# Latent attention scores as three pairs of 64-row products on the two halves of TensorE

## The chip, the cores and the metric

The kernel runs on one core of a Trainium2 chip. The metric is the device time of one execution in microseconds (us), as the median of several. A core has engines that each run their own stream of instructions in order: TensorE (PE in the profile, with its weight loads shown apart as PEld), VectorE (DVE), ScalarE (ACT), GpSimd (POOL) and SyncE (SP), which here issues all DMA transfers. TensorE multiplies a stationary operand, the weights, that is loaded into its array of 128 rows by 128 columns, with a moving operand that is streamed through, and adds up in PSUM. The array's rows are the summed index of a product.

## The reference, cut to what matters

Two layers of a block over 1024 latent and 256 context tokens. In each layer a differential attention runs over 4 heads with 2 maps each (m below), with heads of 64 numbers; its scores, softmaxes and values are what the change touches:

```python
def diff_attention(q, k, v, lam):
    # q (B,Lq,H,2,64), k (B,Lk,H,2,64), v (B,Lk,H,128)
    def one_block(qblk):                      # 128 queries
        s = jnp.einsum('bqhmd,bkhmd->bmhqk', qblk, k).astype(jnp.float32) * scale
        p = jax.nn.softmax(s, axis=-1)
        w = p[:, 0] - lam * p[:, 1]
        return jnp.einsum('bhqk,bkhd->bqhd', w.astype(v.dtype), v)
...
k_all = jnp.concatenate([kc, kx], axis=1)     # 256 context keys, 1024 latent keys
ax = rms_norm(diff_attention(qx, k_all, v_all, lam), p['g_subln']) * (1.0 - lam_init)
...
if ctx_out:                                   # layer 0 only
    ac = rms_norm(diff_attention(qc, kc, vc, lam), p['g_subln']) * (1.0 - lam_init)
```

All inputs are float32. The rest of a layer (one input projection, a state-space scan, a Fourier mixer, an output projection and an MLP) isn't touched.

## The kernel before

The program is one long stretch per stage: input projection, attention, output projection, MLP, twice. Nearly all products of the large stages split each float32 operand into a rounded part (high) and its remainder (low) and multiply these in the one-pass type fp32r, three products for one.

Queries and keys leave the input projection as such pairs. `stack` transposes a block of them, splits it and writes it to DRAM: KD[h, e] holds the keys of head h, part e (0 high, 1 low), with 64 rows of map 0 and 64 rows of map 1, over 1280 columns (1024 latent keys, then 256 context keys); QD[t, e] holds the queries of block t of 128.

The attention reads them back. `load_k(h)` fills two tiles of 128 rows and 1280 columns, ST[h][m] for map m: rows 0 to 63 hold the high part of its keys, rows 64 to 127 the low part. `load_q(t)` fills QS[0] (high) and QS[1] (low), each with the same 64 rows twice, in rows 0 to 63 and 64 to 127. So a product of QS[e] with ST[h][m] over all 128 rows sums the query's part e with both parts of the keys, and two products (e = 0 and 1, `product`, line 654) give all four combinations.

`scores` is called for every block t and head h. It makes the context scores C of both maps (four products of 256 columns), then for each map the latent scores S (line 654 again: two halves of 512 keys, two products each, so four of 512 columns). S is one of two PSUM tiles of two banks, one bank for each half. VectorE takes the maximum over S (line 668), ScalarE the exponential with a running sum (line 670 for S, line 671 for C). `combine` weighs the two maps (line 682, in layer 1 partly on GpSimd, lines 684 and 685). `values` turns the result with ten transposes (line 696), which ScalarE copies out (line 697), and multiplies with V (line 700, float32, so that each of the ten products shows as two in the trace); `finish` (line 714) transposes the outputs. Values lag the scores by three heads. Layer 0 has eight full blocks and two of context queries alone, layer 1 has eight: 2 x 8 x 4 x 2 = 128 maps with latent scores in all.

Beside it run, as fill, the state-space output (`glu`, line 1090, which reads HD back from DRAM, line 1081, after it was written at line 1057) and, in layer 0, part of a modulation product (lines 419 and 427).

Each engine's order is set by a list scheduler, which works over the whole program with costs and dependences; instructions whose costs or number change can come to stand in another order. PE's order is fixed in the program: when its next instruction waits, all behind it wait. SP issues its DMAs in order too.

Elsewhere in the program the state-space setup (lines 917 and 919) already has products of 64 rows, line 917 on rows 0 to 63, line 919 on rows 64 to 127, and line 921 products of 128 rows.

Of the kernel before, what the change touches and what calls it, by code (L numbers as in the profile page):

```python
# [13 lines left out]
F32 = mybir.dt.float32  # L14
# [9 lines left out]
SEQ = 1024  # L24
CTX = 256
TOK = SEQ + CTX
# [41 lines left out]
class Block:  # L68
# [561 lines left out]
    def attention(self, l, V):  # L630
        nc = self.nc
        ST = []

        def load_k(h):
            ST.append([self.s5([128, TOK], F32R) for _ in range(2)])
            for m in range(2):
                for e in range(2):
                    nc.sync.dma_start(ST[h][m][e * 64:e * 64 + 64].bitcast(F32), self.KD[h, e, m * 64:m * 64 + 64])

        def load_q(t, pool='qs'):  # L640
            QS = [self.tl(pool, [128, 2, 4, 128], F32R) for _ in range(2)]
# [7 lines left out]
        def scores(h, t, QS, n):  # L649
            full = t < 8  # L650

            def product(dst, m, a, b):
                for e in range(2):
                    nc.tensor.matmul(dst, QS[e][:, m, h], ST[h][m][:, a:b], start=(e == 0), stop=(e == 1))  # L654

            C = self.pb((128, 2, CTX))
            for m in range(2):
                product(C[:, m], m, SEQ, TOK)
            mx = self.psmall([128, 2, 2], 'mx', 4)
            sm = self.psmall([128, 2, 2], 'es', 5)  # L660
            nc.vector.tensor_reduce(mx[:, :, 0], C, AX.X, ALU.max, negate=True)  # L661
            PR = [E[m][n % 4] for m in range(2)]
            for m in range(2):
                if full:
                    S = self.tl('s', [128, SEQ])
                    for a in (0, 512):
                        product(S[:, a:a + 512], m, a, a + 512)
                    nc.vector.tensor_reduce(mx[:, m, 1:2], S, AX.X, ALU.max, negate=True)  # L668
                    nc.vector.tensor_tensor(mx[:, m, 0:1], mx[:, m, 0:1], mx[:, m, 1:2], ALU.min)  # L669
                    nc.scalar.activation(PR[m][:, 0:SEQ], S, AF.Exp, bias=mx[:, m, 0:1], accum_out=sm[:, m, 1:2])  # L670
                nc.scalar.activation(PR[m][:, SEQ:TOK], C[:, m], AF.Exp, bias=mx[:, m, 0:1], accum_out=sm[:, m, 0:1])
            if full:
                nc.vector.tensor_tensor(sm[:, :, 0], sm[:, :, 0], sm[:, :, 1], ALU.add)  # L673
            return PR, sm
# [43 lines left out]

        pend, done = [], []
        load_k(0)  # L720
        order = range(8) if l == DEPTH - 1 else (0, 1, 2, 8, 3, 4, 9, 5, 6, 7)
        nxt = load_q(0, 'w4')
        for h in range(1, NH):
            load_k(h)
# [3 lines left out]
        for i, t in enumerate(order):  # L728
            QS = nxt
            if i + 1 < len(order):  # L730
                nxt = load_q(order[i + 1])
            AX4 = self.tl('ax' if i + 1 < len(order) else 't2', [128, 4, 128])
            ssq = self.psmall([128, 4], 'ssq', 3)
            for h in range(NH):
                old = pend.pop(0) if len(pend) > 2 else None
                if old is not None:
                    w = combine(*old[:4])
                pend.append((h, t, *scores(h, t, QS, i * NH + h), AX4, ssq, i * NH + h))
                if old is not None:
                    values(*old[:2], *w, *old[4:])  # L740
                if h == 2 and len(done) > 1:
                    finish(*done.pop(0))
                yield
            done.append((t, AX4))
# [698 lines left out]
```

## Time and profile before

| | us |
|---|---|
| median of 3 runs | 3052.49 (3051.86 to 3054.81) |
| the profiled execution, its own time | 3055.69 |
| span of its trace | 3053.9 |
| PE busy | 2907.2 (95%) |
| DVE busy | 1977.9 (65%) |
| ACT busy | 1069.1 (35%) |
| POOL busy | 592.6 (19%) |

The span runs from the first to the last instruction. Busy time is the union of an engine's instructions; matmuls are pipelined, so that one shows some 0.39 us from start to end though the next starts 0.23 us after it. Times between the starts of instructions that follow each other are therefore what counts on PE. The latent scores run from 435 to 684 us (layer 0) and from about 2030 to 2228 us (layer 1).

### The profile page before, as it was taken

The page shows a single profiled execution, that of the slowest core. Times are in us where ns is not written, and L with a number is a line of the kernel's source. Part 1 is how long each engine was busy: PE and PEld are TensorE (multiplying, and loading weights), DVE is VectorE, ACT ScalarE, POOL GpSimd, SP SyncE. Part 2 cuts the span into 40 slices and gives each one's busy share as a digit, 9 for nine tenths or more (in the row PEclk, how much of TensorE's full clock was granted, in tenths as well). Part 3 has the DMA queues.
Part 4 walks back from the last instruction along what each step waited for, and adds up shares of the span by engine and source line. Part 5 has one row for each costly group of instructions (what it writes and reads, how often), then busy time and mean ns, then how long its engine had stood idle before and what let it go on. Part 6 is the DMA issues. An engine that isn't in the chain of part 4 may idle for free. (4 is left out here: it accounts for less than half of the span.)

```text
span 3053.9 us, 40975 instructions
## 1 busy us (share of the span) xinstructions
PE 2907.2 (95%) x15277; PEld 2407.3 (79%) x15277; DVE 1977.9 (65%) x3547; ACT 1069.1 (35%) x2371; POOL 592.6 (19%) x516
## 2 busy tenths in 40 slices
PE   6889989999999999999999999889999999999999
PEld 2557768778888888888888777768889888888887
DVE  7866857785586776775455547858866554455444
ACT  5324437674321211212212433438853222212222
POOL 0643520010100000000465213526621000000000
PEclk9899999999999999999999999999999999999999
DMA  8355483535022322322222235471250111111111
GB/s 291 118 155 158 144 208 121 158 97 162 28 90 78 95 76 83 98 69 61 63 80 70 106 99 153 147 175 49 50 155 29 55 42 56 49 49 42 56 49 66
DMA packets 280851, 299.93 MB, mean 98 GB/s; under 512 B 47158, under 2 KB 191948, under 8 KB 280652
## 3 DMA queue, kind: packets, MB, share of 16 engines
q1 hardware_dynamic: 280652, 297.31, 32.5%
q8 instruction: 120, 1.97, 0.3%
q14 instruction: 79, 0.65, 0.1%
HBM read 229.31 MB, written 67.93 MB: 97 GB/s over the span
## 5 line engine op out<-in xcount | busy, mean ns | idle before, releaser
L1269 PE MATMUL b_t<-hid_t,w_t 128*128 128x512 f32 (+1 forms) x3840 | 809.3, 370 | 0.0
L1246 PE MATMUL b_t<-s_t,w_t 128*128 128x512 f32 (+1 forms) x3840 | 800.4, 369 | 0.0
L1269 PEld LDWEIGHTS b_t<-hid_t,w_t 128*128 128x128 f32 x3840 | 669.6, 189 | 121.8 <-issue 1.9
L1246 PEld LDWEIGHTS b_t<-s_t,w_t 128*128 128x128 f32 x3840 | 669.0, 188 | 121.3 <-issue 1.1
L1271 DVE SCALAR_TENSOR_TENSOR kv_t<-b_t,mod,kv_t 128x512 f32<-128x512 f32 (+1 forms) x640 | 439.4, 694 | 236.6 <-PE b_t L1269 235.6
L159 ACT CAST w_t<-r_t 128x512 fp32r<-128x512 f32 x336 | 195.0, 619 | 807.7 <-PE b_t L1269 526.2
L160 DVE TENSOR_TENSOR w_t<-r_t,w_t 128x512 fp32r<-128x512 f32 x328 | 232.5, 736 | 219.5 <-ACT w_t L159 218.9
L589 PE MATMUL b_t<-w_t,s_t 128*128 128x512 f32 (+1 forms) x1392 | 355.6, 410 | 19.5 <-DVE t_t L478 6.7
L589 PEld LDWEIGHTS b_t<-w_t,s_t 128*128 128x128 f32 x1392 | 264.9, 197 | 83.2 <-issue 9.7
L133 POOL TENSOR_TENSOR sm<-sm,mhalf 128x8 f32<-128x8 f32 (+3 forms) x66 | 103.4, 1567 | 569.6 <-DVE sm L540 191.6
L1250 DVE TENSOR_TENSOR t_t<-b_t,t_t 128x512 f32<-128x512 f32 x160 | 101.2, 633 | 135.6 <-ACT t_t L1249 135.2
L897 POOL TENSOR_TENSOR bg_t<-pt_t,bw_t 128x256 f32<-128x256 f32 x56 | 43.3, 773 | 741.1 <-DMA bw_t<-BD 656.9
L700 PE MATMUL b_t<-kv_t,kv_t 128*128 128x128 f32 x1312 | 178.0, 280 | 3.9 <-ACT kv_t L697 3.4
L700 PEld LDWEIGHTS b_t<-kv_t,kv_t 128*128 128x128 f32 x1312 | 164.2, 193 | 15.0 <-ACT kv_t L697 9.3
L668 DVE TENSOR_REDUCE mx<-s_t 128x1 f32<-128x1024 f32 x128 | 155.2, 1218 | 27.0 <-PE s_t L654 26.5
L159 ACT CAST hid_t<-t_t 128x512 fp32r<-128x512 f32 x160 | 92.4, 578 | 214.0 <-DVE t_t L1250 213.9
L1249 ACT ACTIVATE t_t<-b_t 128x512 f32<-128x512 f32 x160 | 88.3, 552 | 202.3 <-PE b_t L1246 202.3
L670 ACT ACTIVATE s_t<-s_t,mx 128x1024 f32<-128x1024 f32 x128 | 143.6, 1122 | 36.6 <-DVE mx L669 29.0
L160 DVE TENSOR_TENSOR hid_t<-t_t,hid_t 128x512 fp32r<-128x512 f32 x160 | 106.8, 667 | 66.2 <-ACT hid_t L159 66.2
L654 PE MATMUL s_t<-s_t,qs_t 128*128 128x512 f32 x448 | 132.8, 419 | 13.4 <-ACT s_t L670 8.5
L381 DVE SCALAR_TENSOR_TENSOR ac_t<-bg_t,vc,ac_t 128x512 f32<-128x512 f32 x168 | 118.8, 744 | 36.0 <-DMA bg_t<-in_w_mod_dram 35.8
L616 PE MATMUL b_t<-w_t,s_t 128*128 128x512 f32 x480 | 115.6, 395 | 6.7 <-DVE w_t L160 3.5
(335 smaller groups left out, 3506.5 us busy)
## 6 DMA issues: line engine op xcount, KB each, us to landing
r_t<-in_w_ff_dram SPq DMA_DIRECT2D x256, 256.0 KB
bg_t<-in_w_mod_dram SPq DMA_DIRECT2D x96, 256.0 KB
r_t<-in_w_in_dram SPq DMA_DIRECT2D x64, 256.0 KB
qs_t<-QD SPq DMA_DIRECT2D x64, 256.0 KB
XD<-kv_t SPq DMA_DIRECT2D x16, 640.0 KB
KD<-t_t SPq DMA_DIRECT2D x40, 256.0 KB
s_t<-KD SPq DMA_DIRECT2D x32, 320.0 KB
QD<-t_t SPq DMA_DIRECT2D x36, 256.0 KB
```

The source lines that it names most:

```text
L159: self.nc.scalar.copy(h, raw)
L160: (eng or self.nc.vector).tensor_tensor(l, raw, h, ALU.subtract)
L381: nc.vector.scalar_tensor_tensor(acc[v], w, c, acc[v], ALU.mult, ALU.add)
L589: nc.tensor.matmul(p[:, :cols], a[:, ts], W[k][:, b, :cols], start=(n == 0), stop=(n == 23))
L616: nc.tensor.matmul(p, a[:, ts], W[k][:, b], start=(n == 0), stop=(n == 11))
L654: nc.tensor.matmul(dst, QS[e][:, m, h], ST[h][m][:, a:b], start=(e == 0), stop=(e == 1))
L668: nc.vector.tensor_reduce(mx[:, m, 1:2], S, AX.X, ALU.max, negate=True)
L670: nc.scalar.activation(PR[m][:, 0:SEQ], S, AF.Exp, bias=mx[:, m, 0:1], accum_out=sm[:, m, 1:2])
L700: nc.tensor.matmul(o, WT[:, kt * 128:(kt + 1) * 128], V[kt // 5][:, kt % 5, h * 128:(h + 1) * 128], start=(c == 0), stop=(c == len(ks) - 1))
L1246: nc.tensor.matmul(p[:, :w], W[a][:, k], b[k][:, s:s + w], start=(q == 0), stop=(q == 23))
L1269: nc.tensor.matmul(p[:, :w], W[a][:, cs], hid[b][:, s:s + w], start=(q == 0), stop=(q == n - 1))
L1271: nc.vector.scalar_tensor_tensor(xs, p[:, :w], self.mod[l][:, 40 + c, g // 2:g // 2 + 1], xs, ALU.mult, ALU.add)
```

## The change

The latent scores of a map are made of products over 64 rows instead of 128. Per map there are three pairs: query high with key high, query low with key high, query high with key low. The combination of the two low parts, which the kernel before includes, is left out. In each pair the first product uses rows 0 to 63 of the array on keys 0 to 511, the second rows 64 to 127 on keys 512 to 1023; they write the two banks of S. That makes six instructions of 512 columns where there were four, and they are kept in this order.

The keys are laid out for it: of ST[h][e] rows 0 to 63 now hold part e of both maps for latent keys 0 to 511 (map 0, then map 1), rows 64 to 127 the same for keys 512 to 1023. The context columns stay as they were, and so do the context scores. Each of the four loads of a head becomes two: one of 64 rows with two pieces of 512 columns, one of 64 rows with 256 columns.

```diff
         def load_k(h):
             ST.append([self.s5([128, TOK], F32R) for _ in range(2)])
-            for m in range(2):
-                for e in range(2):
-                    nc.sync.dma_start(ST[h][m][e * 64:e * 64 + 64].bitcast(F32), self.KD[h, e, m * 64:m * 64 + 64])
+            for e in range(2):
+                src = self.KD[h, e].rearrange('(m d) c -> d m c', m=2)
+                for r in range(2):
+                    rows = slice(r * 64, r * 64 + 64)
+                    nc.sync.dma_start(ST[h][e][rows, 0:SEQ].rearrange('d (m c) -> d m c', m=2).bitcast(F32),
+                                      src[:, :, r * 512:r * 512 + 512])
+                    nc.sync.dma_start(ST[h][r][e * 64:e * 64 + 64, SEQ:TOK].bitcast(F32), src[:, r, SEQ:TOK])
...
-            def product(dst, m, a, b):
-                for e in range(2):
-                    nc.tensor.matmul(dst, QS[e][:, m, h], ST[h][m][:, a:b], start=(e == 0), stop=(e == 1))
+            def latent(S, m):
+                for q, (e, f) in enumerate(((0, 0), (1, 0), (0, 1))):
+                    for r in range(2):
+                        rows = slice(r * 64, r * 64 + 64)
+                        ins = nc.tensor.matmul(S[:, r * 512:r * 512 + 512], QS[e][rows, m, h],
+                                               ST[h][f][rows, m * 512:m * 512 + 512], start=(q == 0), stop=(q == 2))
+                        if q or r:
+                            self.tc.keep_in_program_order(ins)

             C = self.pb((128, 2, CTX))
             for m in range(2):
-                product(C[:, m], m, SEQ, TOK)
+                for e in range(2):
+                    nc.tensor.matmul(C[:, m], QS[e][:, m, h], ST[h][m][:, SEQ:TOK], start=(e == 0), stop=(e == 1))
...
                     S = self.tl('s', [128, SEQ])
-                    for a in (0, 512):
-                        product(S[:, a:a + 512], m, a, a + 512)
+                    latent(S, m)
```

The scheduler's order moves with it, on PE, DVE and ACT within the two attention stages and on SP at their start. On PE in the middle of layer 1, from the end of one map's latent scores (S, s_t) over ten transposes (line 696, idn) and a head's value products (line 700, kv_t) to the next head's context scores (b_t, 128x256), the rows before are

```order
L654 MATMUL s_t_18933<-s_t_17975,qs_t_18434 128x512
L654 MATMUL s_t_18933<-s_t_17975,qs_t_18435 128x512
L696 MATMUL b_t_18943<-idn_141,s_t_17980 128x128 x2
L696 MATMUL b_t_18947<-idn_141,s_t_17980 128x128 x4
L696 MATMUL b_t_18953<-idn_141,s_t_17980 128x128 x4
L700 MATMUL b_t_18943<-kv_t_17644,kv_t_17988 128x128 x2
L700 MATMUL b_t_18943<-kv_t_17489,kv_t_17988 128x128 x4
L654 MATMUL b_t_18986<-s_t_17950,qs_t_18703 128x256
```

and in the changed program, where all lines from 638 on have moved (654 is 660 for the latent scores and 668 for the context scores, 696 is 705, 700 is 709):

```order
L660 MATMUL s_t_19155<-s_t_18130,qs_t_18626 128x512 x2
L660 MATMUL s_t_19155<-s_t_18130,qs_t_18627 128x512 x2
L660 MATMUL s_t_19155<-s_t_18131,qs_t_18626 128x512 x2
L705 MATMUL b_t_19167<-idn_141,s_t_18140 128x128 x2
L705 MATMUL b_t_19171<-idn_141,s_t_18140 128x128 x4
L705 MATMUL b_t_19177<-idn_141,s_t_18140 128x128 x4
L660 MATMUL s_t_19218<-s_t_18094,qs_t_18911 128x512 x2
L660 MATMUL s_t_19218<-s_t_18094,qs_t_18912 128x512 x2
L660 MATMUL s_t_19218<-s_t_18095,qs_t_18911 128x512 x2
L709 MATMUL b_t_19167<-kv_t_17788,kv_t_18148 128x128 x2
L709 MATMUL b_t_19167<-kv_t_17633,kv_t_18148 128x128 x4
L668 MATMUL b_t_19210<-s_t_18094,qs_t_18911 128x256
```

A map's six products stand together between work of 128 rows, and the next head's first map now comes ahead of the value products and of its own context scores. In the whole program the 768 products of 64 rows stand in 121 such groups, 112 of them with one map, 54 of them followed by a transpose of line 696.

On SP at the start of the attention of layer 0, where the keys of head 0 (s_t) are loaded ahead of the first queries (w_t), before:

```order
L638 DMA s_t_3868<-KD 64x1280 x2
L638 DMA s_t_3869<-KD 64x1280 x2
L646 DMA w_t_3874<-QD 64x2x512 x2
L646 DMA w_t_3875<-QD 64x2x512 x2
L638 DMA s_t_3880<-KD 64x1280 x2
```

and now, the last part of the same stretch:

```order
L642 DMA s_t_3869<-KD 64x256
L640 DMA s_t_3869<-KD 64x2x512
L642 DMA s_t_3868<-KD 64x256
L640 DMA s_t_3869<-KD 64x2x512
L642 DMA s_t_3869<-KD 64x256
L650 DMA w_t_3878<-QD 64x2x512 x2
L650 DMA w_t_3879<-QD 64x2x512 x2
L640 DMA s_t_3884<-KD 64x2x512
```

Eight loads stand where four did, for each of four heads in each layer, with the same bytes; the rest of SP's order there is the same.

## Rows read from the trace of the kernel before

**Rows 1.** The page's part 1: busy us, share of the span, instructions.

```profile
PE 2907.2 (95%) x15277; PEld 2407.3 (79%) x15277; DVE 1977.9 (65%) x3547; ACT 1069.1 (35%) x2371; POOL 592.6 (19%) x516
```

**Rows 2.** Windows, both attention stages: length, busy per engine, granted clock, DMA share, GB/s.

```profile
core 0: us, PE busy (x) PEld busy (x) DVE busy (x) ACT busy (x) POOL busy (x), PEclk, DMA share, GB/s
450.00:700.00 250.00, 231.50 (x1618) 192.17 (x1617) 197.74 (x399) 183.91 (x496) 20.49 (x18) 0.99 0.41 123
2060.00:2230.00 170.00, 164.36 (x1188) 149.84 (x1187) 148.99 (x293) 141.72 (x375) 111.72 (x69) 0.99 0.20 51
```

**Rows 3.** The chain that ended last, layer 1's attention (2060 to 2230 us), by line.

```profile
by line: PE b_t L700 27.8%; PE s_t L654 23.0%; PE b_t L696 11.3%; DVE mx L668 7.8%; PE b_t L654 6.1%; issue 4.6%; DVE s_t L682 4.1%; ACT s_t L670 3.6%; DVE es L673 3.2%; DVE mx L661 2.5%; DVE mx L669 1.6%; PE b_t L714 1.5%; DVE s_t L160 1.0
```

**Rows 4.** Waits of PEld, 430 to 720 us: total us, times, longest.

```profile
PEld s_t L654 <- ACT s_t L670: 11.5, 20, 1.1
```

**Rows 5.** Waits of PEld, 2040 to 2250 us.

```profile
PEld s_t L654 <- ACT s_t L670: 7.9, 10, 1.6
```

**Rows 6.** Timeline of PE, layer 1: start us, us, line, operation, tiles, shape, count.

```profile
2125.62 1.04 PE L696 MATMUL b_t<-idn,s_t 128*128 128x128 f32 x8
2126.41 1.17 PE L654 MATMUL s_t<-s_t,qs_t 128*128 128x512 f32 x4
2127.42 1.50 PE L700 MATMUL b_t<-kv_t,kv_t 128*128 128x128 f32 x12
2128.75 0.60 PE L714 MATMUL b_t<-idn,ax_t 128*128 128x128 f32 x4
```

**Rows 7.** Groups by form, whole span: count, busy us, mean ns, idle before.

```profile
L1269 PE MATMUL b_t<-hid_t,w_t 128*128 128x512 f32 x3072 | 715.2, 392 | 0.0
```

**Rows 8.** Timeline of PE, state-space setup beside the input projection, layer 0.

```profile
120.17 0.62 PE L589 MATMUL b_t<-w_t,s_t 128*128 128x512 f32 x2
120.73 0.36 PE L917 MATMUL f_t<-bg_t,bw_t 64*16 64x112 f32 x2
...
121.84 0.94 PE L919 MATMUL f_t<-bg_t,bw_t 64*16 64x112 f32 x8
122.71 0.21 PE L921 MATMUL f_t<-bw_t 128*16 128x16 f32 x2
```

**Rows 9.** The same, a little earlier, where lines 917 and 919 alternate.

```profile
117.74 0.27 PE L917 MATMUL f_t<-bg_t,bw_t 64*16 64x112 f32 x1
117.75 0.27 PE L919 MATMUL f_t<-bg_t,bw_t 64*16 64x112 f32 x1
117.85 0.26 PE L917 MATMUL f_t<-bg_t,bw_t 64*16 64x112 f32 x1
117.86 0.26 PE L919 MATMUL f_t<-bg_t,bw_t 64*16 64x112 f32 x1
...
118.43 0.50 PE L589 MATMUL b_t<-w_t,s_t 128*128 128x512 f32 x1
```

**Rows 10.** Line 654's own view, latent scores: ns shortest/median/longest.

```profile
L654 PE MATMUL s_t<-s_t,qs_t x448: 387/397/774, 467.2 to 2227.3; 128*128 128x512 f32 x150
```

**Rows 11.** Timeline of PE: transposes right after a product of 64 rows.

```profile
104.71 0.26 PE L919 MATMUL f_t<-bg_t,bw_t 64*16 64x112 f32 x1
104.89 0.66 PE L910 MATMUL f_t<-idn,bg_t 128*128 128x128 f32 x4
```

**Rows 12.** Timeline of SP, start of layer 0's attention: start us, us, DMA issues.

```profile
403.23 15.39 SPq L638 DMA_DIRECT2D s_t<-KD  x12
...
422.85 5.99 SPq L646 DMA_DIRECT2D qs_t<-QD  x5
429.71 8.70 SPq L1057 DMA_DIRECT2D HD<-kv_t  x8
```

**Rows 13.** Timeline of PE there; in brackets idle us before, and its releaser.

```profile
444.71 2.08 PE L1090 MATMUL b_t<-kv_t,w_t 128*128 128x512 f32 x2 [7.29 <-DMA kv_t<-HD]
```

**Rows 14.** Windows, layer 1: a stretch and the one after it (columns as in rows 2).

```profile
2068.10:2071.50 3.40, 1.37 (x7) 1.05 (x8) 2.86 (x7) 2.38 (x7) 1.29 (x2) 1.00 0.01 2
2071.50:2074.90 3.40, 3.40 (x17) 3.12 (x16) 3.00 (x5) 2.21 (x6) 2.73 (x2) 0.51 0.00 0
```

## The prediction

> **What bounds the kernel now.** The page's shares come first: PE is busy 95% of the span and no other engine over 65% [rows 1], so work taken from PE counts unless the stage has another limit. The change lies in two stages, and the windows over them say which: in layer 1 PE is busy 164.4 of 170 us, DVE 149.0, ACT 141.7; in layer 0 231.5 of 250, 197.7 and 183.9 [rows 2]. PE bounds both, but closely followed. The chain of waits in layer 1 runs over PE for some 70% of its length (values 27.8, latent scores 23.0, transposes 11.3, context scores 6.1, outputs 1.5) and for the rest mostly over the maximum, the exponential and the weighing of the maps [rows 3]. So I let 0.7 of what PE gains or loses reach the end. Third, who makes PE wait: the load of weights for a latent score stood waiting for the exponential that frees one of the two S tiles 20 times in layer 0 and 10 times in layer 1, 19.4 us in all [rows 4, 5]. At some 90 of 120 places PE came to the latent scores without waiting.
>
> **What a map costs now.** From eight transposes at 2125.62 over four products to the values at 2127.42 is 1.80 us; four transposes that start at 2128.75 take 0.60, of which 0.27 is the last one's run out, so one follows another after 0.11, and the four products hold PE for 1.80 - 0.88 = 0.92, 0.23 each [rows 6]. The MLP's products agree: 715.2 us for 3072, 0.233 each [rows 7]. That spacing has the next weights loaded behind the product in flight. Nothing is lost at the borders of a group now.
>
> **The change, part by part.**
>
> *One product less per map.* If the two products of a pair run at once, a map takes three spacings for four: 128 x 0.233 = 29.8 us less on PE. That they do run at once, this kernel shows: where lines 917 and 919 alternate on the two halves, each 919 starts 0.01 us after its 917, and the next pair 0.10 after the first [rows 9]; eight of line 919 alone take (0.94 - 0.26)/7 = 0.097 each [rows 8]. A pair costs one product. Those products are float32 of 112 columns with 16 columns of weights; that 512 columns of fp32r behave alike is carried over.
>
> *Going into a group.* The same rows show what the diff doesn't: at the border between 128 and 64 rows PE stops. From the second product of line 589 (120.17 + 0.23) to the first of line 917 (120.73) it is 0.33 instead of 0.23; from the first of eight of line 919 to line 921 it is 0.87 where 8 x 0.097 = 0.78 would do [rows 8]. Each border costs 0.09. And nothing is loaded ahead over it: the first product after such a border lasts 0.50 us [rows 9], against a median of 0.40 for those in the stream [rows 10], so 0.11 (0.10 to 0.11) for its 128 columns of weights lies open. The second half adds its offset of 0.01. Together 0.21 per group, 121 groups in the changed order: 25.4 us. Where PE waits at the entry for the S tile anyway, the stop is covered, and the weights lay open there already: 30 x 0.20 = 6.0 off [rows 4, 5]. If that cover goes because PE itself becomes later, the 6.0 come back.
>
> *Coming out.* The second border costs 121 x 0.09 = 10.9. Behind it the next weights lie open again: for a transpose 0.06, by the four transposes after a product of 64 rows (0.66 us, against 0.60 in the stream) [rows 6, 11], for values and context scores 0.11 as above: 54 x 0.06 + 67 x 0.11 = 10.6. Together 21.5.
>
> *Sum on PE:* -29.8 + 25.4 - 6.0 + 21.5 = +11.1 us; with 0.7 of it on the path, +7.8. The three kinds of border cost alone outweigh the product saved: 0.21 + 0.09 + 0.06 to 0.11 is 0.36 to 0.41 per group, against 0.233 for one map.
>
> *Key loads.* Sixteen more DMAs per layer, in front of other work on SP. Behind them stand the second queries, the eight writes of HD and its read [rows 12], for which PE waits 7.29 us in layer 0 [rows 13]. SP issues twelve key loads in 15.39 us, 1.28 us for 320 KB, and five query loads (256 KB, pieces of 512 columns) in 5.99, 1.20 each [rows 12]: 250 against 213 KB/us. If the new loads move at the lower rate, 16 x 320 KB take 24.0 instead of 20.5 us, 3.5 more per layer; if piece size doesn't matter, nothing. The first loads lie well ahead of their use. I take 1.5 per layer, since those five also waited for other things: +3 (0 to 7), all of it on the path.
>
> *The order.* On PE the next head's first map now stands before the value products and its own context scores. It waits for the S tile that the exponential of the map before the last frees. I cost this at nothing: PE has other work in the same places, and the two maps alternate as before; if DVE then reduces late, a few of the 30 waits move. I allow 3 us either way.
>
> *Base.* The profiled execution took 3055.69 us, of which its span is 3053.9; the median is 3.2 lower. 3055.69 + 7.8 + 3 = 3066.5 on it, 3063 on the median.
>
> **The rivals.**
>
> *Latency decides, and it is a wash.* From the freed S tile to the finished map it was 4 x 0.23 = 0.92, behind open weights; now 0.70 behind the same. At the 30 waits the maximum can start 0.22 earlier, 6.6 us, while the costs of coming out fall on PE where ACT and DVE set the pace. For it: 30% of the chain on the softmax [rows 3], DVE busy 88% in layer 1 [rows 2]. Against: PE is at 97% there, and 91 groups have no wait to win. -6.6 + 3 gives 3049. Chance 0.21.
>
> *The full gain.* If two borders cost less than 128 x 0.233 / 121 = 0.25 per group, PE gains; at nothing it is -29.8 x 0.7 + 3, 3035. Both border prices were read where the columns of weights also differ (16 against 128), so a change of rows alone could be cheaper. Against it: the transposes after line 919 [rows 11] start 0.18 after it instead of 0.10, the same stop for any successor. Chance 0.08.
>
> *Weights don't hide inside a group.* If in the 64-row form the weights of the second and third pair wait for the product that runs in the same half, two loads of 0.11 lie open per group: 121 x 0.22 = 26.6, 0.7 of it 18.6, which gives 3082. Against: eight of line 919 on one half follow each other after 0.097, no more than the alternating pairs [rows 8, 9], and 128-row products hide theirs [rows 7]; for it, that line 919's 16 columns of weights are too few to show much. The Trainium skill (TensorE: Matmul & The Clock Gate, Part 3) states that a weight load overlaps with products in flight only where its row group differs; by that rule this rival holds, and the trace's 128-row stream of 0.233 us speaks against it. A cost of the same size could come from the granted clock: after a stretch with PE busy 1.37 of 3.40 us it stood at 0.51 in the next, about the lower level of 1.2 GHz [rows 14]; each such stretch costs up to 1.7 us, and a few more are possible. Chance 0.12.
>
> *The halves don't run at once.* Six spacings per map: 128 x 3 x 0.233 = 89.5 more, near 3150. [Rows 9] speak plainly against it: 0.02.
>
> **How the numbers follow.** Forecast 0.57, wash 0.21, open weights or clock 0.12, full gain 0.08, no pairs 0.02. The range reaches from 3045, within the wash, to 3083, which takes in the third rival's middle; it leaves out the full gain, the missing pairs and some 0.09 of the others. About 0.2%, 6.1 us, is what a measurement of this kernel can tell from no change: 3046.4 to 3058.6. Faster: full gain 0.08 and 0.06 of the wash, 0.14. Same: 0.15 of the wash and the forecast's lower edge, 0.12, so 0.27. Slower: 0.45 + 0.12 + 0.02 = 0.59.
>
> **What would show it.** In the trace after, the latent groups' second product of a pair should start about 0.01 us after the first, and pairs 0.23 apart: right for the pairing. From the last product of 128 rows to the first of a group 0.09 more than its stream, and the first pair's spacing near 0.34: right for the way in; the transposes or values 0.32 after the last pair's start: right for the way out. If pairs follow at 0.34, the third rival holds; if nothing is lost at the borders, the second. PE's waits on the exponential should fall below 19 us. The wait for HD should grow from 7.29 by one or two us. The forecast is wrong if the groups are as costly as said and the stages still don't grow: then PE didn't bound them.

## The result, and the profile after

The changed kernel takes 3076.2 us (3074.7 to 3078.0), the kernel before 3051.9 in the same comparison: a ratio of 1.008 (95%: 1.0069 to 1.0091), 24.4 us slower. The prediction was 3063, slower, with a range to 3083. The sign and the range held; the size was more than twice the +10.5 forecast.

The page of the profile after, part 1 (answers to [rows 1]):

```profile
PE 2920.9 (95%) x15533; PEld 2378.0 (77%) x15533; DVE 1980.5 (64%) x3547; ACT 1068.2 (35%) x2371; POOL 590.4 (19%) x516
```

PE is busy 13.7 us more, over a span that is 21.8 us longer (3075.7); the other engines' work is the same. The rest must lie in the two stages. From the first latent score to the last, the windows of the kernel before are

```profile
435.00:683.70 248.70, 223.94 (x1510) 182.42 (x1509) 189.21 (x384) 174.97 (x473) 17.95 (x16) 0.97 0.44 130
2029.70:2227.30 197.60, 182.62 (x1253) 161.03 (x1252) 164.34 (x318) 154.00 (x404) 117.58 (x72) 0.97 0.24 63
```

and those of the changed kernel (columns as in [rows 2]: length, then the busy time of PE, PEld, DVE, ACT and POOL)

```profile
432.80:693.60 260.80, 231.55 (x1641) 169.99 (x1642) 191.93 (x383) 174.11 (x472) 18.10 (x16) 0.96 0.42 125
2041.10:2252.50 211.40, 190.28 (x1379) 146.49 (x1380) 164.24 (x321) 153.14 (x402) 116.00 (x73) 0.98 0.22 58
```

12.1 and 13.8 us longer: 25.9 together, which covers all of the loss. PE's busy time in them has grown by 15.3, its idle time by 10.6. The 15.3 are not the price of the new products: the old products in the same order (an experiment below) keep PE busy for 419.4 us in the two stages, where the kernel before has 406.6 and the changed kernel 421.8. The clock isn't the cause either: the granted clock over the whole execution is 0.985 before and 0.984 after.

Inside a group of 64-row products everything is as the prediction drew it. The timeline of PE, layer 1, after (answers to [rows 6]; L705 are transposes, L660 latent scores, L709 values, L668 context scores):

```profile
2140.47 0.38 PE L705 MATMUL b_t<-idn,s_t 128*128 128x128 f32 x2
2140.78 0.96 PE L660 MATMUL s_t<-s_t,qs_t 64*128 64x512 f32 x6
2141.67 1.09 PE L705 MATMUL b_t<-idn,s_t 128*128 128x128 f32 x8
...
2147.82 1.31 PE L705 MATMUL b_t<-idn,s_t 128*128 128x128 f32 x10
2150.13 0.97 PE L660 MATMUL s_t<-s_t,qs_t 64*128 64x512 f32 x6 [1.00 <-ACT s_t L679]
2151.04 1.60 PE L709 MATMUL b_t<-kv_t,kv_t 128*128 128x128 f32 x12
```

Two transposes at 0.11 would let a 128-row successor start after 0.22; the group starts after 0.31, so the border costs 0.09. From the group's first product to the next transpose it is 0.89, which is the 0.34 + 0.23 + 0.32 of the prediction. (In the instructions one by one, the two products of a pair start 0.002 to 0.004 us apart, the pairs 0.34 and then 0.23. Over the 110 groups of a single map that ran at the full clock the medians are 0.337 and 0.231, and 0.327 from the last pair to the next product.) What is not as drawn is the second group: PE waited 1.00 for the exponential (L679), with twelve value products queued behind. This wait, which was to become rarer, is the one that grew. Waits of PE in the two stages, 430 to 740 and 2040 to 2290 us (total, times, longest):

```profile
PE s_t L660 <- ACT s_t L679: 9.8, 17, 1.5
...
PE s_t L660 <- ACT s_t L679: 10.5, 15, 1.1
```

Before they were 4.7 us (9 times) and 5.2 (6 times):

```profile
PE s_t L654 <- ACT s_t L670: 4.7, 9, 0.7
...
PE s_t L654 <- ACT s_t L670: 5.2, 6, 1.4
```

The chain of waits, 2110 to 2180 us, says more (answers to [rows 3]):

```profile
by line: ACT s_t L679 27.3%; ACT kv_t L706 18.2%; ACT s_t L680 13.8%; issue 12.8%; DVE s_t L691 8.9%; DVE mx L671 5.6%; ACT jk_t L713 3.4%; DVE es L682 2.6%; DVE rr L688 2.4%; DVE rr L689 1.9%; DVE mx L678 1.6%; DVE ax_t L711 1.1%; DVE sm L
...
2124.44 1.23 ACT kv_t L706 x3
...
2150.54 1.23 ACT kv_t L706 x3
...
2176.62 1.24 ACT kv_t L706 x3
```

Before, some 70% of it was PE [rows 3]. Now it runs between ACT (exponentials L679 and L680, copies of transposes L706) and DVE (maximum of the context L671, sum L682, weighing L691), and PE is not in it. It repeats with every block of four heads, after 26.10 and 26.08 us. The chain of the kernel before repeats as well, with PE's value products (L700), after 24.22 and 24.21 us:

```profile
2151.81 1.34 PE b_t L700 x12
...
2176.03 1.34 PE b_t L700 x12
...
2200.24 1.34 PE b_t L700 x12
```

By the starts of the latent groups, too, the period of a block in the middle of layer 1 is 24.2 us before and 26.1 after. In these two kernels it is constant to a few hundredths, so it is a finer measure than the whole time, and the experiments below are read by it too.

The timelines of DVE and ACT show what a turn of that loop is made of. DVE:

```profile
2140.14 0.16 DVE L682 TENSOR_TENSOR es<-es 128x2 f32<-128x2 f32 x1 [1.01 <-ACT s_t L680]
2140.22 0.68 DVE L671 TENSOR_REDUCE mx<-b_t 128x2 f32<-128x512 f32 x1
2140.82 0.15 DVE L688 RECIPROCAL rr<-es 128x2 f32<-128x2 f32 x1
2140.94 0.16 DVE L678 TENSOR_TENSOR mx<-mx 128x1 f32<-128x1 f32 x1
```

and ACT:

```profile
2139.88 0.23 ACT L680 ACTIVATION_READ_ACCUMULATOR s_t<-b_t,mx 128x1 f32 x1
2141.21 1.11 ACT L679 ACTIVATE s_t<-s_t,mx 128x1024 f32<-128x1024 f32 x1 [1.10 <-DVE mx L678]
```

DVE stands idle 1.01 us until ACT has the last map's exponential sum; then ACT stands idle 1.10 us until DVE has the next map's minimum. Each waits for the other in turn.

### The profile page after: what moved, and what is told of

It is laid out like the page before. It is cut to its first block, busy times and chain, and to the rows that moved or that the text cites. A ratio compares the mean times of both kernels' runs of the same rounds, so it can differ in the third digit from the quotient of the medians.

```text
span 3075.7 us, 41533 instructions
## 1 busy us (share of the span) xinstructions
PE 2920.9 (95%) x15533; PEld 2378.0 (77%) x15533; DVE 1980.5 (64%) x3547; ACT 1068.2 (35%) x2371; POOL 590.4 (19%) x516
## 4 chain that ended last, share of the span: by engine, by line
PE 70%; DVE 10%; ACT 5%; DMA 5%; issue 2%; POOL 1%; SPq 1%; DVEq 0%; ACTq 0%; POOLq 0%
PE b_t L1255 26%; PE b_t L1278 25%; PE b_t L1222 7%; PE b_t L589 4%; ACT s_t L679 2%; PE b_t L709 2%; DVE s_t L691 1%; DMA s_t<-KD 1%; DVE mx L677 1%; ACT s_t L680 1%; ACT kv_t L706 1%; PE f_t L1138 1%; DMA qs_t<-QD 1%; PE s_t L660 1%; DMA r_t<-in_w_in_dram 1%
## 5 line engine op out<-in xcount | busy, mean ns | idle before, releaser
L589 PEld LDWEIGHTS b_t<-w_t,s_t 128*128 128x128 f32 x1392 | 263.8, 196 | 82.4 <-issue 10.8
L709 PE MATMUL b_t<-kv_t,kv_t 128*128 128x128 f32 x1312 | 184.1, 283 | 6.9 <-ACT kv_t L706 6.5
L709 PEld LDWEIGHTS b_t<-kv_t,kv_t 128*128 128x128 f32 x1312 | 162.6, 193 | 31.8 <-ACT kv_t L706 21.0
L679 ACT ACTIVATE s_t<-s_t,mx 128x1024 f32<-128x1024 f32 x128 | 143.7, 1122 | 72.7 <-DVE mx L678 70.1
L660 PE MATMUL s_t<-s_t,qs_t 64*128 64x512 f32 x672 | 112.5, 434 | 22.0 <-ACT s_t L679 18.4
```

What stands on the lines that cost most here:

```text
L589: nc.tensor.matmul(p[:, :cols], a[:, ts], W[k][:, b, :cols], start=(n == 0), stop=(n == 23))
L660: ins = nc.tensor.matmul(S[:, r * 512:r * 512 + 512], QS[e][rows, m, h], ST[h][f][rows, m * 512:m * 512 + 512], start=(q == 0), stop=(q == 2))
L709: nc.tensor.matmul(o, WT[:, kt * 128:(kt + 1) * 128], V[kt // 5][:, kt % 5, h * 128:(h + 1) * 128], start=(c == 0), stop=(c == len(ks) - 1))
```

## The experiments

Two things changed at once, the products (with their loads) and the order of the instructions. So the first four runs hold the order fixed. Orders are held by dependences that only set the order of issue, on PE, DVE, ACT and POOL within each attention stage; a map's latent products count as one unit.

**New products, old order.** On the changed kernel:

```diff
+    def pin(self, l, at):
+        stage = self.nc.cur_bb.bb.instructions[at:]
+        for eng, runs in ORDER[l].items():
...
+            for a, b in zip(row, row[1:]):
+                self.tc.add_manual_dep(b, a.name, mybir.DependencyInfo(
+                    mybir.DependencyClass.NoSync, mybir.DependencyReason.DATA), reason='pin')
```

with ORDER the kernel before's.

> The change's 64-row pairs and key loads, with PE, DVE, ACT and GpSimd held in the kernel before's order in both attention stages (a map's six products stand where its four stood). Theory 1 (the borders cost what the trace shows, some 11 us net on PE, and the moved order costs the rest of the 24): 3060 to 3066 us, and PE's waits on the exponential near those of the kernel before. Rival (the order is innocent, all 24 come from the borders because PE bounds the stages more than thought): 3074 to 3078, as with the change's own order.

Measured 3055.07, ratio 1.0029 (1.0018 to 1.0040), against 3047.68 for the kernel before on this chip. That is below both ranges and nearer the first: the loss, 8.8 us by the ratio (7.4 by the medians), is a third of the changed kernel's. PE waits 2.0 and 4.1 us for the exponential; the block takes 24.7 us, 0.5 more than before.

**Old products, new order.** The same edit on the kernel before, with ORDER the changed kernel's.

> The kernel before's four products of 128 rows and its key loads, with the four engines held in the changed program's order. Theory 1 (the order costs some 13 us by itself): 3060 to 3068 us, with PE waiting for the exponential longer than before at the groups that moved ahead of the value products. Rival (the order is innocent): 3050 to 3055.

Measured 3077.44, ratio 1.0102 (1.0087 to 1.0118). Not one product is different from the kernel before, and it is as slow as the changed kernel; the block takes 26.1 us, as there. So the order alone costs 31 us by the ratio, where 13 were expected. Both stages pay for it (windows from the first latent score to the last):

```profile
429.60:690.90 261.30, 229.30 (x1517) 185.10 (x1516) 191.83 (x384) 174.36 (x473) 18.12 (x16) 0.96 0.42 125
2033.40:2251.60 218.20, 190.13 (x1256) 162.58 (x1254) 164.47 (x322) 153.97 (x403) 116.69 (x73) 0.97 0.22 58
```

Its chain, 2060 to 2230 us:

```profile
by line: ACT s_t L833 25.5%; issue 13.6%; ACT kv_t L860 13.2%; ACT s_t L834 12.5%; DVE s_t L845 9.6%; DVE mx L824 5.3%; DVE mx L831 4.1%; ACT jk_t L867 3.0%; DVE mx L832 2.7%; DVE es L836 2.5%; DVE rr L842 2.4%; DVE rr L843 2.2%; DVE w_t L3
```

The same loop, with other line numbers (L833 is the exponential, L834 that of the context, L860 the copies, L845 the weighing). Since none of PE's products is in it behind 2070 us, four long ones or three pairs give the same period.

**Four pairs, and three products, in the old order.** What does a spacing on PE bring when nothing moves? One run adds a pair to the new products:

```diff
-                for q, (e, f) in enumerate(((0, 0), (1, 0), (0, 1))):
+                for q, (e, f) in enumerate(((0, 0), (1, 0), (0, 1), (1, 1))):
```

> As new_products_old_order, with a fourth pair per map, low by low, so that the streaming time per map is that of the kernel before and the borders alone remain (all four combinations are computed again). If 0.7 of PE's time reaches the end: 128 x 0.233 x 0.7 = 21 us over new_products_old_order; if all of it does: 30; if the softmax decides: under 10. Over the kernel before it should be the whole price of the borders, 0.38 per group: 28 to 46 us.

Measured 3073.39, ratio 1.0087 (1.0074 to 1.0101): 18.3 us over the three pairs for 29.8 on PE, a share of 0.6. Over the kernel before it is 25.7, just under the 28 to 46 expected. The other takes a product from the old ones (the low part of the queries on keys 512 to 1023 is left out):

```diff
-                for e in range(2):
+                n = 1 if a == 512 else 2
+                for e in range(n):
```

> The kernel before in its own order, with three products of 128 rows per map instead of four: keys 512 to 1023 lose the product of the query's low part, which leaves its part out of those scores. It is the change's saving without any border. If 0.7 of PE's time reaches the end: 29.8 x 0.7 = 21 us less, 3031; if all of it does: 3022; if the softmax decides: 3042 to 3052.

Measured 3045.45, ratio 0.9987 (0.9978 to 0.9996): 4 us (1.2 to 6.7) for 29.8. What is added on PE lands to 0.6, what is taken away to 0.13. The block in layer 1 says the same less sharply: of the 1.86 us of its eight spacings a fourth pair adds 1.4 to the period and a product less takes off 0.6, shares of 0.7 and 0.3. With a product less PE waits more: its idle time in the two stages is 10.9 us longer, and its waits for the exponential rise from 4.7 and 5.2 to 7.5 and 6.5 us. Even the full saving with no borders at all would have been worth some 4 us in this order.

**The loads alone.** On the kernel before, in its own order:

```diff
-                    nc.sync.dma_start(ST[h][m][e * 64:e * 64 + 64].bitcast(F32), self.KD[h, e, m * 64:m * 64 + 64])
+                    dst, src = ST[h][m][e * 64:e * 64 + 64].bitcast(F32), self.KD[h, e, m * 64:m * 64 + 64]
+                    dst, src = (x.rearrange('d (a c) -> d a c', a=2) for x in (dst, src))
+                    nc.sync.dma_start(dst[:, :, 0:512], src[:, :, 0:512])
+                    nc.sync.dma_start(dst[:, :, 512:640], src[:, :, 512:640])
```

> The kernel before in its own order, with each of the sixteen key loads of a layer made as two, one of 64 rows with two pieces of 512 columns and one of 64 rows with 256 columns. The prediction's step says +3 us (0 to 7) and a wait for HD of 8 to 9.5 us in place of 7.3 in layer 0 and likewise in layer 1: ratio 1.000 to 1.002. If piece size doesn't matter, the ratio is 1.000 and the wait stays within 0.5 us of what it was.

Measured 3054.57 against 3047.9, ratio 1.0022 (1.0013 to 1.0031): +6.7 us (4.0 to 9.4), the upper part of the range and not the wait I named: PE waits 7.6 and 7.8 us for HD, as before. The period of a block is unchanged (24.2), so the loss is not in the steady blocks. (The kernel before with its own order held and nothing else changed was not run; what holding costs, if anything, is in the 6.7.) In layer 0 PE waits 5.6 us for queries (2.8 before). From the first key load to the last latent score it is 3.5 us more in layer 0 and 1 in layer 1; the rest of the 6.7 I have not placed. On SP a load takes its time by its number more than by its bytes. The changed kernel, layer 0 (answers to [rows 12]):

```profile
394.74 0.62 SPq L640 DMA_DIRECT2D s_t<-KD x1
395.41 0.60 SPq L642 DMA_DIRECT2D s_t<-KD x1
```

256 KB (L640) and 64 KB (L642) hold SP for 0.6 us each, as the first four of 320 KB did before (2.41 us together). That this is how the loads cost 6.7 us is not shown.

**Which place in the order?** My first reading was the place that the prediction's section on the change had shown: a next head's first map stands ahead of the value products and holds them up. So these maps were moved behind, on PE alone, in the changed kernel's own order:

```diff
 eight or ten transposes (L705)
-latent scores of a map (L660)
 value products (L709)
+latent scores of a map (L660)
```

> The changed kernel, held in its own order on every engine, except that on TensorE each map's latent products that stand right between transposes and value products (37 maps, 11 in layer 0 and 26 in layer 1) are moved behind those value products. If the moved order costs what it does because such a map waits for the exponential that frees its S tile and holds up the value products behind it, the waits on the exponential (9.8 and 10.5 us in the two stages) fall below 8 us in all and the ratio to the kernel before comes from 1.008 down to 1.003 to 1.005. If the cost sits elsewhere in the order (which engine reduces or copies what first), the ratio stays above 1.006.

Measured 3118.41, ratio 1.0229 (1.0215 to 1.0243). The waits for the exponential did fall, to 5.1 and 3.2, but the values now waited for the copies of their transposes. PE, layer 1 (L869 values, L866 copies):

```profile
PE b_t L869 <- ACT kv_t L866: 28.5, 28, 2.0
```

3.0 us in the changed kernel. The latent scores had been the cover for these copies. The block now takes 30.9 us. So the waits at this place are not where the time can be got back with PE alone; what the place costs when the other engines' orders fit it, the run doesn't tell.

**PE in the old order, the rest in the new.** On the changed kernel, with ORDER mixed.

> The changed kernel with TensorE in the order of the kernel before, and VectorE, ScalarE and GpSimd in the order of the changed kernel. If TensorE's order is what costs, this is like the run with all four in the old order: ratio 1.002 to 1.004. If the order of VectorE and ScalarE carries the cost, it stays at 1.007 or more. A mixture of two orders that were not made for each other can also cost something of its own; a ratio in between would say so.

Measured 3149.63, ratio 1.033 (1.0316 to 1.0344), worse than either order. In the two stages PE's value products wait 35.8 us for copies, its latent scores 20.0 for the exponential and its transposes 20.7 for DVE. These two orders don't go together; the run doesn't tell whose share is the larger.

**Fewer borders.** Both maps of a head together, to halve the groups: PE in the old order, with the first map's products moved to the second's, the other engines free.

> The changed products with TensorE held in the order of the kernel before, but the first map's latent products of a head moved to stand right ahead of the second map's; the other engines are ordered freely around it. That makes 64 groups of 64-row products where there were some 120, so some 57 fewer at 0.21 going in and 0.17 coming out: 21 us less on TensorE, and with 0.6 of it on the path some 13 us less than the changed products in the old order (3055): about 3042, ratio 0.998. The rival: a group now needs both S tiles free at its start, so that TensorE waits for the second map's exponential at every head; then the ratio is 1.003 or more and the waits on the exponential exceed 20 us.

Measured 3122.13, ratio 1.0242 (1.0229 to 1.0256). The rival holds: 30.6 us of waits for the exponential, and 31.7 of the value products for copies.

**The sum on DVE.** The second reading: the wait of DVE shown above, 23.0 us in layer 1 where it was 4.7. DVE's waits for the exponential sums, 2040 to 2290 us, in the kernel before, the changed kernel and the first of the two runs that follow:

```profile
DVE es L673 <- ACT s_t L671: 4.7, 7, 0.8
...
DVE es L682 <- ACT s_t L680: 23.0, 26, 1.1
...
DVE es L843 <- ACT s_t L841: 8.7, 15, 1.0
```

On the changed kernel, in its own order, DVE alone:

```diff
 maximum of the next head's first map (L677)
-sum of the last head's exponential sums (L682)
 maximum of the next head's context scores (L671)
-reciprocal (L688)
 minimum of the two (L678)
+sum of the last head's exponential sums (L682)
+reciprocal (L688)
```

> The changed kernel, held in its own order on every engine, except on VectorE at 17 places (3 in layer 0, 14 in layer 1): there the sum of a head's two exponential sums (line 682) stands right behind the next head's first maximum (line 677) and ahead of that map's context maximum and minimum (lines 671, 678); now it stands behind them. In the changed kernel VectorE is idle ahead of line 682 for 35.1 us at 47 places, against 16.9 at 17 before, and the exponential of the next map waits for line 678 queued behind it. If this queue is where the moved order costs, the idle time ahead of line 682 falls by some 15 us, the next exponential starts some 0.8 us earlier at 17 places, and the ratio to the kernel before comes from 1.008 to 1.004 or 1.005. If VectorE's queue only waits where the chain would wait anyway, the ratio stays at 1.007 or more.

> The same at all 40 places (13 and 27) where the sum (line 682) stands between a next head's first maximum and its minimum, also where the reciprocal and the weighing of the maps (lines 688, 689, 691) stand between them. At the 23 further places the context maximum (line 671) may have to wait for its context scores, which TensorE makes behind the value products, and the weighing then comes later. If the exponential of the next map is what is late, the ratio is 1.002 to 1.005; if the delayed weighing holds up the transposes, it is above that of the 17 places, 1.006 or more.

At 17 places: 3074.2, ratio 1.0081 (1.0067 to 1.0095). The wait ahead of the sum fell from 23.0 to 8.7 us in layer 1 and the block from 26.1 to 25.4, but the time can't be told from the changed kernel's. At 40 places: 3091.13, 1.0138 (1.0124 to 1.0152), as the second branch said; DVE there waits 22.3 us in layer 1 for the context scores. So this queue is a part of the loop, a third of what a block has lost, and not the whole cause.

**A third order.** The scheduler counts a 64-row product like one of 128, so it plans six in a row where the chip runs three pairs. That this count is what moved the order is a guess which no run here shows. Handed three products of 128 rows per map it makes a third order, and both kinds of products were run in that.

> The changed kernel held, on TensorE, VectorE, ScalarE and GpSimd, in a third order: the one in which the scheduler itself places the kernel before when each map has only three of its four products of 128 rows, so that it counts a map's latent scores at three products and not at six. If the scheduler's count of six products where the chip runs three pairs is what made the changed kernel's order poor, this order serves the new products at least as well as the old one (3055, ratio 1.003): 0.998 to 1.003, with waits on the exponential of 8 us or less in all. If the order is a matter of luck, of which the kernel before has had a good draw, this one is no better than the changed kernel's own: 1.006 or more.

> The kernel before, with its four products of 128 rows per map, in the same third order. It tells how good that order is apart from the products: with the old products the kernel's own order gives 1.000 and the changed kernel's gave 1.010. Between the old and the new products the old order showed 8.8 us and the new order -1. If the third order is good, the old products in it come to 0.997 to 1.003, and the new ones to some 9 us more or less; if it is poor, to 1.006 or more.

New products: 3048.92, ratio 1.0004 (0.9995 to 1.0013). Old products: 3038.13, ratio 0.997 (0.9959 to 0.9981), faster than both kernels. PE of the latter, layer 1 (L860 transposes, L816 latent scores and, with 256 columns, context scores, L864 values):

```profile
2123.36 0.72 PE L816 MATMUL b_t<-s_t,qs_t 128*128 128x256 f32 x4
2123.93 1.05 PE L864 MATMUL b_t<-kv_t,kv_t 128*128 128x128 f32 x8
2124.82 0.38 PE L860 MATMUL b_t<-idn,s_t 128*128 128x128 f32 x2
2124.95 1.18 PE L816 MATMUL s_t<-s_t,qs_t 128*128 128x512 f32 x4
2125.97 0.60 PE L860 MATMUL b_t<-idn,s_t 128*128 128x128 f32 x4
2126.33 1.18 PE L816 MATMUL s_t<-s_t,qs_t 128*128 128x512 f32 x4
2127.34 0.60 PE L860 MATMUL b_t<-idn,s_t 128*128 128x128 f32 x4
2127.78 1.50 PE L864 MATMUL b_t<-kv_t,kv_t 128*128 128x128 f32 x12
```

This is one head, and in the steady blocks of layer 1 three of four look like it: context scores first, both maps of a head behind them, four transposes apart. No first map of layer 1 stands ahead of its own context scores, where 14 of the 28 heads behind the first block did before and 25 do in the changed kernel. (Such a map's exponential can't start before the context's maximum.) The chain, 2060 to 2215 us, is PE's again:

```profile
by line: PE b_t L864 33.1%; PE s_t L816 28.0%; PE b_t L860 16.1%; PE b_t L816 7.1%; issue 3.6%; DVE mx L832 3.0%; ACT s_t L834 2.4%; PE b_t L878 1.4%; ACT s_t L835 0.9%; DVE mx L833 0.9%; DVE mx L825 0.8%; DVE s_t L846 0.7%; DVE s_t L322 0.
```

The old products gain by it too, though they are four and not three: the truer count is not all that makes an order good. Which of its features does it no run has taken apart.

All of it in one table (ratio to the kernel before, and the period of a block in layer 1, us):

| order | old products | new products | new less old |
|---|---|---|---|
| the kernel before's | 1.000, 24.2 | 1.0029, 24.7 | +8.8 us |
| the changed kernel's | 1.0102, 26.1 | 1.008, 26.1 | -6.7 us |
| the third | 0.997, 23.2 | 1.0004, 24.0 | +10.4 us |

The last column is taken from the ratios. Those of the second row come from two comparisons; their difference, 0.0022, is little more than the half width of either interval (0.0011 and 0.0016), so the -6.7 is hardly clear of nothing.

## Why the prediction was right in sign and short in size

**The pairs, and the product saved: right.** A pair costs one spacing, here 0.23 for 512 columns of fp32r, as it did for the 112 columns of float32 from which this was carried over [rows 9]. The rival without pairs falls.

**Going in and coming out: right.** 0.09, open weights and 0.32 on the way out, each as read from [rows 6, 8, 9, 11]. The rival in which the borders are free falls. The Trainium skill (TensorEngine Tiling (Array Packing), Key Properties) states that changing the tiling mode drains TensorE; the rows agree, with 0.09 us each way.

**Weights inside a group: right.** The third pair follows the second at 0.23, and the second the first at 0.34, as drawn for the open weights of the first pair alone. The second and third pair load into the rows that are in use, and nothing of that lies open; the rival in which it does falls. The Trainium skill (TensorE: Matmul & The Clock Gate, Part 3) states that a weight load overlaps with products in flight only where its row group differs; here the trace differs from it. The clock, the other half of that rival, stayed as it was (0.985 and 0.984).

**The sum on PE: right in sign, and near in size.** +11.1 forecast, that is 0.7 per block of a layer (16 in all). With the order held, PE's busy time over both stages rises by 8.4 us in the old order (406.6 to 415.0) and by 5.9 in the third (404.6 to 410.5), and the period of a block in layer 1 by 0.5 and 0.9.

**The products and loads together: right as a sum, in orders that let PE set the pace.** +10.8 forecast, +8.8 and +10.4 measured. How it divides is less clear. The loads were put at 3 and cost 6.7 (4.0 to 9.4), and not by the wait for HD, which stayed at 7.6 and 7.8 us in that run (in the changed kernel itself it is 8.7 and 5.6, where 7.3 and 7.9 were before). By subtraction some 2 to 4 us are left for the products, where 7.8 was said; by the period of a block, which the loads leave alone, they cost 3.8 and 7.0 us over the eight blocks of layer 1 if all were like the steady ones. The intervals allow both. The landing share of 0.7 holds for work that is added (0.6 measured), not for work that is taken away (0.13). I took one share for both signs, from a chain of which 30% was not PE; that a faster PE runs into that 30% is argued, from its longer waits for the exponential.

**The order: the step that failed.** "I cost this at nothing: PE has other work in the same places, and the two maps alternate as before", with 3 us either way. The same old products lose 31 us by the order alone. The argument looked at PE's neighbours at one place. It didn't follow the next map's way round: its exponential needs its context's maximum, whose scores now come later, and DVE and ACT, whose own orders had moved as well, then wait for each other in turn. This way round is read from the timelines and the count of heads above; no run has changed it by itself. The sentence on the waits fell with it: they were to sink below 19 us on the weight loads and went to 31.1 (16.2 and 14.9). The last sentence of the prediction comes near the case: costly groups, but a stage that PE doesn't bound. Here the stage grew and PE no longer bounded it.

**What was luck.** That 3076 lies within the range: its part above 3063 was there for weights that don't hide and for the clock, and neither came. And in the order that was run the products and loads added nothing (-6.7, hardly clear of nothing), so that the sign, too, came from the term put at nothing; with the order held it would have been the same, for the reasons given.

**The wash: not shown.** Its mechanism, a shorter way from the freed tile to the finished map, should show where PE waits anyway. In the changed kernel's order the new products come out 6.7 us faster than the old, close to its estimate of 6.6; but a block takes 26.1 us with either. In the traces the new products save 6.4 us of layer 1, and 4.9 of them lie in its first block (32.0 us against 37.0, from its first latent product to the next block's). So the likeness of the two numbers is no evidence for it.

Open is which of the moved rows in PE's, DVE's and ACT's orders carries the most of the 31 us. Moving single rows told of parts of the loop (0.7 of 1.9 us per block on DVE's sum), and moved the wait elsewhere.

## What to carry to other kernels

Where a scheduler sets the order, changing the number or kind of instructions can change the order of everything beside them, and here that cost three times what the instructions did; hold the order fixed, and cost the two apart. A saving on the busiest engine can be worth far less than the same time added to it costs: ask for the two shares separately. And try the orders that a scheduler makes from other costs: the one made for three products per map in place of six took the new products from 1.008 to 1.0004, and the old ones, which are four, to 0.997.

## What was not expected of the hardware

A fourth pair on PE cost 0.6 of its time and a product less gave back 0.13 of its own (0.7 and 0.3 by the period of a block), in the same order. PE was busy some 13 us longer in the two stages with the same products in another order, so busy time alone doesn't price a change of products. A DMA issue on SP takes 0.6 us for 64 KB as for 256 KB, and sixteen more per layer cost 6.7 us in all.
